# A streaming encoder step: gate and residual of the second MLP applied behind the last but one group of its down projection

## The chip, the cores and the metric

The kernel runs on one core of a Trainium2 chip. A core has TensorE (matrix products into PSUM, 8 banks), VectorE, ScalarE and GpSimd (element-wise work), and SyncE, whose queue issues most of the DMAs; GpSimd and ScalarE can issue DMAs too. 16 DMA engines carry the transfers of all queues. The metric is the device time of one execution, in microseconds. In the profile PE is TensorE, DVE is VectorE, ACT is ScalarE, POOL is GpSimd, SP is SyncE; L1443 is line 1443 of the kernel, and a group is written "out<-in" with the program's names for tiles.

## The reference, cut to what matters

One inference step of a two-layer encoder on 1056 tokens (1024 of a prompt and 32 of a sample, each of the two with its own conditioning), 1024 features, 4096 hidden features in the MLP. Each layer ends with a squared-ReLU MLP whose result is scaled by a gate per feature and condition and added to the residual, before a layer norm:

```python
u = x * (1 + sc2) + sh2
f = jnp.square(jax.nn.relu(u @ p['w_up'][l])) @ p['w_down'][l]
x = layer_norm(ALPHA * x + (1 + g2) * f, p['ln_g'][l, 1], p['ln_b'][l, 1])
```

Here `g2` differs between the 1024 prompt tokens and the 32 sample tokens. Everything is float32; the kernel computes products as three passes over a high and a low part of each operand. The factor 1/ALPHA is folded into the gate, so that in the kernel the sum is `x + gate * f`.

## The kernel before, in words

Features lie on partitions, tokens along the free dimension. An accumulator `ACX` of two tiles, four blocks of 128 features each (index `fc`, 0 to 7), holds all 1056 tokens. Tokens are cut into four quarters of `QN` = 264; the last quarter holds the last 232 prompt tokens and the 32 sample tokens.

The second MLP (`mlp7(L1)`) runs the hidden features in 16 blocks of 256. For the first 14 the products are made by a scheme of seven products in place of eight (`PRODS`): per product a weight form (from `forms`: sums and differences of quarter blocks of the weights, split into a high and a low part) and a form of the hidden activations, which the up projection has written to DRAM (`hd`). The last two blocks are multiplied plainly at the end.

The down projection of the 14 blocks goes in five groups (`GRP`, of 2, 3, 3, 3 and 3 blocks, numbered 0 to 4) of four units each; a unit `(g, m)` makes two feature blocks, `fc` = 2m and 2m+1, for all tokens: seven products times two halves of the tokens (`tp`), fourteen in all, each of 9 matmuls of 264 columns in groups 1 to 4. Their sums stay in PSUM banks within the unit (`unit`, L1428 to 1449). After each product one quarter of one feature block is complete enough to be taken out: `L.raw` (that is `add_raw_at`) copies it into `ACX` on ScalarE for the first product that touches the place (group 0), and adds it there on VectorE otherwise (L1066, one instruction of 128 x 264). The bank is free again when that is done.

What goes on beside a unit:

- `step` calls `advance` after each product: the weights of the next units are loaded (`rdn_d`, two loads of 384 KB a unit, L1256, on SyncE's queue), added and subtracted on VectorE (L1272 to 1275) and split by ScalarE's cast (L89) and VectorE's subtraction (L90) into `wf_d`. The loads go through a ring of three buffers, the split weights through one of six.
- in the last unit of a group, `after` hands the place of each used activation form to the next group's (`fill`, `rooms`): its DMA (`fx`, `fx_e`, `fx_w`, L1124, 792 KB for each of the fourteen operands, in one or two pieces) goes onto SyncE's queue behind the product that frees the place. A few operands are loaded earlier into free places.
- after each unit of the last group, 4, `L.fold` (that is `gate_raw`) is called for the two feature blocks: ScalarE multiplies them by the gate (L1073: 1024 prompt columns, then 32 sample columns), and an accumulating DMA on GpSimd's queue (L1074, 528 KB) adds the residual from DRAM (`xsp[2]`) to them.

Behind the last unit the remaining two blocks are multiplied plainly (L118 to 120, `dn_plain`'s counterpart at the end of `mlp7`): operands `hs` (four loads of 1056 KB, L1553), weights `w_dn` (four loads of 512 KB, L96), and each product goes into `ACX` by `L.add` (that is `add_gated_at`, L1057): `ACX = product * gate + ACX`, on VectorE, one instruction for each condition that the columns cover. Then the layer norm and the output follow, token block by token block.

The order on TensorE is written out by hand (`manual_schedule`). On the other engines the instructions are ordered by the framework's planner from the order of the program and its own costs; each engine and each queue then works in that order, and a waiting instruction holds what is behind it.

Of the kernel before, what the change touches and what calls it, by code (L numbers as in the profile page):

```python
# [75 lines left out]
def trunk_kernel(ctx: ExitStack, tc: tile.TileContext, a, o):  # L76
# [100 lines left out]
    def tpt(name):  # L177
        return pa.tile([P, 512], F32, tag="tp", name=name, bufs=2)
# [27 lines left out]
    tp = tpt("tp_c")  # L206
# [13 lines left out]
    tp = tpt("tp_p2")  # L220
# [876 lines left out]
    QN = T // 4  # L1097
    NPB, KG = 16, 4
    GRP = [(0, 2), (2, 3), (5, 3), (8, 3), (11, 3)]
# [31 lines left out]
    def mlp7(L):  # L1131
# [212 lines left out]
        def advance(n, i):  # L1344

            if n + 1 in preps and i in (0, 1, 3, 5):
                got[n + 1] = next(preps[n + 1])
            if i == 2:
                prep(n + 2)
            if not NW and n == len(seq) - 1 and i in (1, 3):  # L1350
                w_plain(0, i // 2)
# [65 lines left out]
        def fill(g, into, most=99):  # L1417

            kg = GRP[g][1]
            while want and len(rooms.free) >= kg and most:  # L1420
                most -= 1
                if g >= len(GRP) - 3:
                    late = g == len(GRP) - 1 or g == len(GRP) - 2 and len(into) < 10
                    rooms.free.sort(key=lambda r: any(r[0] is t for t in f4s[:3]) == late)
                tp, f = want.pop(0)
                into[tp, f] = rooms.load(hd[g][tp][f], kg)

        def unit(g, m, phases, ws, step, after):  # L1428


            kg = GRP[g][1]
            for tps in phases:
                ps = {}
                for i, (w, f, b, c, q) in enumerate(PRODS):
                    for tp in tps:
                        first = (tp, b) not in ps
                        if first:
                            ps[tp, b] = mm(f"dn{l}_{g}_{m}_{tp}_{b}")
                        p = ps[tp, b][:, :QN]
                        for k in range(kg):  # L1440
                            t, s0 = fx[tp, f][k]
                            for n_, (wl, xl) in enumerate(((0, 0), (0, 1), (1, 0))):
                                nc.tensor.matmul(p, ws[w][:, wl, k], t[:, s0, xl], start=first and k + n_ == 0,  # L1443
                                                 stop=k == kg - 1 and n_ == 2, skip_group_check=not first)
                        L.raw((2 * tp + q) * QN, QN, p, 2 * m + c, g == 0 and i in (0, 2, 3, 6))
                        after(tp, f)
                        flow.tick(QN * kg / 768)
                    if tps is phases[-1]:
                        step(i)
# [16 lines left out]
        with tc.manual_schedule(engines={mybir.EngineType.PE}):  # L1466
            for _, j, i in sorted((7 * j + 2 * i, j, i) for j in range(len(jobs)) for i in range(7)):
                n, tp = jobs[j]
# [53 lines left out]
        with tc.manual_schedule(engines={mybir.EngineType.PE}):  # L1522
            for i, (g, m, phases) in enumerate(units):
                more = g + 1 < len(GRP)
                if i == 0:
                    rooms.add(ring.tile([P, KG, 2, QN], F32R, tag="wc", name=f"fx_w{l}", bufs=6))
                    fill(0, fx)
                if m == 1 and more:
                    want += [(tp, f) for f in order_f for tp in L.pairs]
                if g and m == 2 and more:  # L1530
                    fill(g + 1, nfx)

                def after(tp, f):
                    if m == 3 and more:
                        rooms.free += fx[tp, f]
                        fill(g + 1, nfx)

                def step(j):
                    advance(nu + i, j)
                    if g == 0 and m in (1, 2):  # L1540
                        fill(g + 1, nfx, 1)
                unit(g, m, phases, got[nu + i], step, after)
                if not more:
                    for fc in (2 * m, 2 * m + 1):
                        L.fold(L.gate, fc, xsp[2])
                if m == 3:
                    assert not want
                    fx, nfx = nfx, {}
# [68 lines left out]
    class L0:  # L1617
# [46 lines left out]
        def after(blk):  # L1664
# [3 lines left out]
            norms[ti] = flow.add(norm(ti, 1, f"n01_{ti}", W01[ti], False, lambda ti: acc_dma(  # L1668
                xsp[1][:, :, t0:t0 + n], acc[ti], True)), now=NOW)
    mlp7(L0)  # L1670


# [8 lines left out]
    for gi, grp in enumerate(((0, 1, 2), (3,))):  # L1681
        ws = {pr: [wblock(f"q{pr}_{half}", wq, 512 * half, 256 * pr) for half in range(2)] for pr in grp}
        for ti, (t0, n) in enumerate(TBS):
# [9 lines left out]
            for fc in [f for pr in grp for f in (2 * pr, 2 * pr + 1)]:  # L1693
                g, r = fc // 2, 2 * (fc % 2)
# [217 lines left out]
    for gp in range(2):  # L1912
        for i in range(17):
            c = slim[gp][i // 2] if i % 2 else wide[i // 2] if i < 16 else slim[gp][8]
            if not gp and i < 2:
                c = 7 + i
# [18 lines left out]
    for t in range(NT):  # L1935
# [4 lines left out]
        m = P if t < NT - 1 else TS  # L1940
# [124 lines left out]
    class L1:  # L2065
# [49 lines left out]
        def after(blk):  # L2115
            t0, n = blk
            tiles = [(t, min(P, t0 + n - t)) for t in range(t0, t0 + n, P)]
            flow.add(norm_out(tiles, L1.put_out, L1.next_y, L1.gb, blk == L1.blocks[-1]), TAIL[0])
    mlp7(L1)
    flow.finish()  # L2120
    psD_cm.__exit__(None, None, None)
# [36 lines left out]
```

## Time and profile before

| | us |
|---|---|
| median of 3 runs (2407.66 to 2410.68) | 2410.06 |
| the profiled execution | 2410.77 |
| its span, first to last instruction | 2409.0 |
| TensorE busy | 2341.5 (97%) |
| VectorE busy | 1935.2 (80%) |
| ScalarE busy | 1206.4 (50%) |
| GpSimd busy | 176.3 (7%) |

The mean granted clock of TensorE is 0.995 of full speed. Of the profile these views are used: the page; rows of stretches of time (busy time of each engine with its count of instructions, then the granted clock `PEclk`, the share of the 16 DMA engines and what they moved in GB/s); timelines (start, duration, engine, line, operation, and in brackets how long the engine was idle before it and what ended that); the chain of waits that ended last (start, duration, what); and the DMA view (a queue with its packets, megabytes and share of 16 engines; an issue with its size and the time to landing). q1 is the queue of SyncE's DMAs, q0 that of GpSimd's. A busy TensorE is modelled, so its rows tell when it stood still, and the length of a unit tells how fast it was.

The last group's folds stand in the profile at 2283.7 to 2340.0 (ScalarE, 16 activations) and 2288.1 to 2341.6 us (GpSimd, 8 DMAs); the plain blocks begin at 2339.3.

### The profile page before, as it was taken

Reading aid. Unit: us, or ns where it says so; the run is one execution under the profiler, and the core shown is the slowest. Engines: PE = TensorE matmul, PEld = TensorE weight load, DVE = VectorE, ACT = ScalarE, POOL = GpSimd, SP = SyncE. Lnnn points to the kernel's source line nnn. Section 1 sums busy time; section 2 is a strip of 40 time slices with the busy share of each in tenths; the row PEclk is TensorE's granted clock in tenths of the full one; section 3 lists DMA queues with packets and bytes.
Section 4 is the critical chain, followed back from the end, with each engine's and each line's share of the span. In section 5 each row is a group of like instructions: output and inputs, shape, how many; then the busy total and the mean of one; then the engine's idle time right before and its main releaser. Section 6 shows DMA issues by size and latency. Waiting matters only on the chain. (4 is left out here: it accounts for less than half of the span.)

```text
span 2409.0 us, 44246 instructions
## 1 busy us (share of the span) xinstructions
PE 2341.5 (97%) x17180; PEld 2250.1 (93%) x17180; DVE 1935.2 (80%) x3982; ACT 1206.4 (50%) x2442; POOL 176.3 (7%) x323
## 2 busy tenths in 40 slices
PE   7999999999999999999999999999999999999997
PEld 4999999999999999999989987789999999999997
DVE  4899897778788789989888677757998889677658
ACT  4644457278566631000147467764766777422232
POOL 0211100000000000000000224420000000000013
PEclk9999999999999999999999999999999999999999
DMA  8333322526566896675512230051586789866672
GB/s 302 120 113 95 100 84 79 173 97 203 182 202 198 287 350 238 226 272 204 177 62 88 77 93 1 19 134 56 175 279 207 254 279 313 328 244 240 237 191 74
DMA packets 284854, 424.65 MB, mean 176 GB/s; under 512 B 15448, under 2 KB 205292, under 8 KB 280036
## 3 DMA queue, kind: packets, MB, share of 16 engines
q1 hardware_dynamic: 279284, 387.15, 48.5%
q10 hardware_dynamic: 4208, 30.35, 3.2%
q0 software_dynamic: 1152, 4.33, 1.0%
q8 instruction: 135, 2.21, 0.4%
q14 instruction: 75, 0.61, 0.1%
HBM read 305.96 MB, written 118.17 MB: 176 GB/s over the span
## 5 line engine op out<-in xcount | busy, mean ns | idle before, releaser
L1443 PE MATMUL dn<-fx,wf_d 128*128 128x264 f32 x2016 | 254.7, 286 | 6.9 <-DVE ACX L1066 3.1
L1443 PEld LDWEIGHTS dn<-fx,wf_d 128*128 128x128 f32 x2016 | 250.0, 189 | 8.5 <-issue 3.0
L89 ACT CAST w_dn<-raw_dn 128x1024 fp32r<-128x1024 f32 x36 | 37.7, 1050 | 285.1 <-DMA raw_dn<-in_w_down_dram 111.8
L1057 DVE SCALAR_TENSOR_TENSOR ACX<-dn,ada,ACX 128x384 f32<-128x384 f32 (+5 forms) x304 | 136.9, 469 | 40.0 <-PE dn L120 37.2
L118 PE MATMUL dn<-hs,w_dn 128*128 128x384 f32 (+2 forms) x512 | 160.9, 315 | 0.0
L119 PE MATMUL dn<-hs,w_dn 128*128 128x384 f32 (+2 forms) x512 | 160.9, 315 | 0.0
L120 PE MATMUL dn<-hs,w_dn 128*128 128x384 f32 (+2 forms) x512 | 156.4, 314 | 1.3 <-DVE w_dn L90 1.3
L1066 DVE TENSOR_TENSOR ACX<-dn,ACX 128x264 f32<-128x264 f32 x248 | 104.4, 429 | 62.3 <-PE dn L1443 60.9
L1308 PE MATMUL up<-TF,wf_u 128*128 128x264 f32 x1056 | 143.2, 285 | 4.1 <-ACT H L1311 4.1
L1308 PE MATMUL up<-U,wf_u 128*128 128x264 f32 x1056 | 139.6, 285 | 1.1 <-DVE H L1314 0.7
L1308 PE MATMUL up<-u,wf_u 128*128 128x264 f32 x1056 | 139.4, 284 | 1.2 <-DVE H L1314 0.8
L277 DVE SCALAR_TENSOR_TENSOR aw<-radw,cs,aw 128x512 f32<-128x512 f32 x196 | 139.3, 742 | 1.4 <-DMA radw<-in_w_ada_dram 1.4
L1308 PEld LDWEIGHTS up<-TF,wf_u 128*128 128x128 f32 x1056 | 134.2, 188 | 5.1 <-ACT H L1311 5.1
L1308 PEld LDWEIGHTS up<-U,wf_u 128*128 128x128 f32 x1056 | 133.1, 188 | 2.1 <-DVE H L1314 1.3
L1308 PEld LDWEIGHTS up<-u,wf_u 128*128 128x128 f32 x1056 | 132.5, 188 | 1.8 <-DVE H L1314 1.2
L118 PE MATMUL dn<-U,w_dn 128*128 128x384 f32 (+2 forms) x416 | 129.4, 312 | 0.9 <-DVE ada L302 0.9
L119 PE MATMUL dn<-U,w_dn 128*128 128x384 f32 (+2 forms) x416 | 129.8, 313 | 0.0
L120 PE MATMUL dn<-U,w_dn 128*128 128x384 f32 (+2 forms) x416 | 125.5, 312 | 0.4 <-DVE w_dn L90 0.4
L1811 ACT ACTIVATE p<-p,mx 128x576 f32<-128x576 f32 (+9 forms) x132 | 86.5, 656 | 27.1 <-DVE mx L1808 24.9
L90 DVE TENSOR_TENSOR HL<-H,HL 128x1056 fp32r<-128x1056 f32 x64 | 80.3, 1254 | 22.7 <-ACT HL L89 22.3
L120 PEld LDWEIGHTS dn<-hs,w_dn 128*128 128x128 f32 x512 | 95.9, 188 | 2.1 <-DVE w_dn L90 1.7
L119 PEld LDWEIGHTS dn<-hs,w_dn 128*128 128x128 f32 x512 | 96.5, 188 | 0.0
(399 smaller groups left out, 7249.2 us busy)
## 6 DMA issues: line engine op xcount, KB each, us to landing
hpl<-HL SPq DMA_DIRECT2D x144, 264.0 KB
rdn_u<-in_w_up_dram SPq DMA_DIRECT2D x64, 512.0 KB
hd<-HL SPq DMA_DIRECT2D x28, 1056.0 KB
fx<-hd SPq DMA_DIRECT2D x50, 528.0 KB
radw<-in_w_ada_dram SPq DMA_DIRECT2D x24, 1024.0 KB
hd<-HM SPq DMA_DIRECT2D x28, 792.0 KB
raw_up<-in_w_up_dram SPq DMA_DIRECT2D x40, 512.0 KB
raw_dn<-in_w_down_dram SPq DMA_DIRECT2D x36, 512.0 KB
```

Source lines behind the costliest of these rows:

```text
L89: nc.scalar.copy(dst_h, src)
L90: (eng or nc.vector).tensor_sub(dst_l, src, dst_h.bitcast(F32))
L118: nc.tensor.matmul(ps, wh, mov(0, k), start=(k == 0), stop=False)
L119: nc.tensor.matmul(ps, wh, mov(1, k), start=False, stop=False)
L120: nc.tensor.matmul(ps, wl, mov(0, k), start=False, stop=(k == nk - 1))
L277: nc.vector.scalar_tensor_tensor(acc[cnd], raw[:, k], sc, acc[cnd], op0=ALU.mult, op1=ALU.add)
L1057: nc.vector.scalar_tensor_tensor(xs, ps[:, off + o:off + o + mm_], gate[:, fc, cnd:cnd + 1], xs, op0=ALU.mult, op1=ALU.add)
L1066: nc.vector.tensor_add(x[:, fc], ps[:, off:off + m], x[:, fc])
L1308: nc.tensor.matmul(p, self.ws[w][:, wl, k], moving(f, tp, xl, k), start=first and k + n_ == 0, stop=k == 3 and n_ == 2, skip_group_check=n ...
L1443: nc.tensor.matmul(p, ws[w][:, wl, k], t[:, s0, xl], start=first and k + n_ == 0, stop=k == kg - 1 and n_ == 2, skip_group_check=not first)
L1811: nc.scalar.activation(z, z, AF.Exp, bias=mx[:, 0:1], scale=-1.0, accum_out=mx[:, 1:2])
```

## The change

The fold of a pair of feature blocks is called behind the unit of group 3 that makes them, and no longer behind that of group 4. At that time `ACX` holds the sum of groups 0 to 3, so gate and residual are applied to this; the products of group 4 are then added with the gate, by the function that the plain blocks use. In the last quarter of the tokens that function issues two instructions (232 and 32 columns), so that four of a unit's fourteen additions become two each.

```diff
                                 nc.tensor.matmul(p, ws[w][:, wl, k], t[:, s0, xl], start=first and k + n_ == 0,
                                                  stop=k == kg - 1 and n_ == 2, skip_group_check=not first)
-                        L.raw((2 * tp + q) * QN, QN, p, 2 * m + c, g == 0 and i in (0, 2, 3, 6))
+                        if g < len(GRP) - 1:
+                            L.raw((2 * tp + q) * QN, QN, p, 2 * m + c, g == 0 and i in (0, 2, 3, 6))
+                        else:
+                            L.add((2 * tp + q) * QN, QN, p, L.gate, 2 * m + c)
                         after(tp, f)
...
                 unit(g, m, phases, got[nu + i], step, after)
-                if not more:
+                if g == len(GRP) - 2:
                     for fc in (2 * m, 2 * m + 1):
                         L.fold(L.gate, fc, xsp[2])
```

The two functions called, as they were:

```python
def add_gated_at(t0, n, ps, gate, fc):
    for off, m, x in pieces(t0, n):
        for o, mm_, cnd in segs(t0 + off, m):
            xs = x[:, fc, o:o + mm_]
            nc.vector.scalar_tensor_tensor(xs, ps[:, off + o:off + o + mm_], gate[:, fc, cnd:cnd + 1], xs,
                                           op0=ALU.mult, op1=ALU.add)

def gate_raw(gate, fc, src):
    x = acc["all"].tiles[fc // 4][:, fc % 4]
    for off, m, cnd in segs(0, T):
        xs = x[:, off:off + m]
        nc.scalar.activation(xs, xs, AF.Copy, scale=gate[:, fc, cnd:cnd + 1])
    nc.gpsimd.dma_start(x, src[:, fc], accum_op=ALU.add)
```

## The prediction

> **What bounds the kernel now.** First the page of the kernel before: its span, its engines, and the group of additions that the change is about.
>
> ```profile
> span 2409.0 us, 44246 instructions
> PE 2341.5 (97%) x17180; PEld 2250.1 (93%) x17180; DVE 1935.2 (80%) x3982; ACT 1206.4 (50%) x2442; POOL 176.3 (7%) x323
> L1066 DVE TENSOR_TENSOR ACX<-dn,ACX 128x264 f32<-128x264 f32 x248 | 104.4, 429 | 62.3 <-PE dn L1443 60.9
> ```
>
> TensorE sets the pace, so an edit counts only where it lengthens or shortens a unit of the second down projection. I write (g,m) for group g, unit m; the change touches groups 3 and 4, the last two. A unit without a stall is 126 matmuls in 15.36 us. Counting back from the last matmul of (4,3), whose end is at 2339.4, the view of stretches gives one row for each of the eight units, (3,0) to (4,3):
>
> ```profile
> core 0: us, PE busy (x) PEld busy (x) DVE busy (x) ACT busy (x) POOL busy (x), PEclk, DMA share, GB/s
> 2211.45:2226.81 15.36, 15.36 (x129) 15.36 (x128) 12.03 (x28) 3.40 (x7) 0.00 (x0) 1.00 0.84 327
> 2226.81:2242.17 15.36, 15.36 (x129) 15.36 (x128) 11.67 (x27) 3.29 (x7) 0.00 (x0) 1.00 0.57 193
> 2242.17:2257.53 15.36, 15.36 (x129) 15.36 (x128) 10.87 (x25) 3.29 (x7) 0.00 (x0) 1.00 0.18 52
> 2257.53:2272.89 15.36, 15.36 (x129) 15.36 (x128) 9.37 (x21) 3.30 (x7) 0.00 (x0) 1.00 0.97 351
> 2272.89:2288.25 15.36, 15.36 (x129) 15.36 (x128) 11.51 (x26) 5.10 (x10) 0.19 (x1) 1.00 0.94 354
> 2288.25:2307.25 19.00, 17.43 (x129) 17.03 (x128) 12.05 (x28) 5.93 (x11) 1.72 (x2) 0.91 0.75 213
> 2307.25:2322.61 15.36, 15.36 (x129) 15.36 (x128) 9.37 (x21) 6.05 (x11) 1.92 (x3) 1.00 0.62 140
> 2322.61:2339.41 16.80, 15.56 (x128) 15.37 (x127) 9.97 (x18) 6.95 (x8) 1.57 (x2) 1.00 0.76 198
> ```
>
> Six units run at the pace; (4,1) is 3.64 us longer and (4,3) 1.44 us, 5.08 us together, and those are the two stalls that can be won. The timeline of VectorE (first three rows), of GpSimd, of the DMA queue of SyncE and the chain of waits tell what they hang on:
>
> ```profile
> 2275.50 0.55 DVE L1272 TENSOR_TENSOR s_d<-rdn_d,rdn_d 128x384 f32<-128x384 f32 x1
> 2300.97 0.56 DVE L1272 TENSOR_TENSOR s_d<-rdn_d,rdn_d 128x384 f32<-128x384 f32 x1 [4.53 <-DMA rdn_d<-in_w_down_dram]
> 2335.34 1.23 DVE L90 TENSOR_TENSOR w_dn<-raw_dn,w_dn 128x1024 fp32r<-128x1024 f32 x1 [3.45 <-ACT w_dn L89]
> ...
> 2288.06 1.04 POOL L1074 DMA_DIRECT2D ACX<-xsp  x1 [693.38 <-ACT ACX L1073]
> 2290.65 0.86 POOL L1074 DMA_DIRECT2D ACX<-xsp  x1 [1.54 <-ACT ACX L1073]
> 2325.16 0.86 POOL L1074 DMA_DIRECT2D ACX<-xsp  x1 [1.84 <-ACT ACX L1073]
> ...
> 2291.62 9.26 DMA rdn_d<-in_w_down_dram
> 2325.04 9.12 DMA raw_dn<-in_w_down_dram
> 2135.37 5.40 DMA rdn_d<-in_w_down_dram
> ```
>
> The chain is one of data: in (4,1) a 384 KB weight load issued at 2291.62 takes 9.26 us, where the same load took 5.40 us earlier in the phase; VectorE stands 4.53 us at the head of its queue waiting for it (L1272), the additions that empty the PSUM banks stand behind it, and TensorE runs out of banks. In (4,3) a 512 KB load takes 9.12 us, ScalarE's cast of it is late, and VectorE idles 3.45 us. Beside each late load run two accumulating DMAs of the fold (the folds of (4,0) at 2288.06 and 2290.65, one of (4,2) at 2325.16). What a fold takes of the DMA engines is in the DMA view from 2288 to 2301 (first four rows), and what plain loads take in the one from 2259 to 2282.5 (last row):
>
> ```profile
> q1 hardware_dynamic: 999, 2.33, 55.7%
> q0 software_dynamic: 288, 1.08, 41.8%
> hs<-hpl SPq DMA_DIRECT2D x2, 1056.0 KB
> ACX<-xsp POOLq DMA_DIRECT2D x2, 528.0 KB, 9.6
> ...
> q1 hardware_dynamic: 3603, 8.81, 101.1%
> ```
>
> 41.8% of 13 us is 5.43 us of all 16 engines for two folds: 2.7 us each, 5.0 us per MB. 101.1% of 23.5 us over 8.81 MB is 2.7 us per MB for plain loads. A fold therefore costs nearly twice its bytes, and whatever load shares the engines with two of them is up to 5.4 us late.
>
> **The change part by part.** *The folds move up by one group.* The 8 folds (16 activations on ScalarE, 8 DMAs on GpSimd's queue) are issued 61.4 us (4 x 15.36) before where they would stand without stalls, one pair behind each of (3,0) to (3,3). By the offset of the pair of (4,0) from its unit's start (15.2 and 17.8 us), the pairs are then issued at about 2226.6/2229.2, 2242.0/2244.6, 2257.4/2260.0 and 2272.7/2275.3. ScalarE has room: busy 3.3 us of 15.36 in these units. GpSimd's queue holds nothing else there.
>
> *Group 4 loses them.* The load at 2291.62 and that at 2325.04 get the engines back. 9.26 less up to 5.4 is 3.9, so the nearest value is the 5.40 us of the quiet one: landing some 4 us sooner, the 4.53 us wait is nearly gone, and 9.12 less one or two folds takes the 3.45 us off too. I take the whole 5.08 us as won; the lower end is 3.64, if (4,3) stalls for its 1 MB `hs` load and not for the fold.
>
> *(3,3) and (4,0) get them.* These are the units in which the operands of group 4 are loaded, and the DMA is full there: share 0.97 and 0.94 above. SyncE's queue in that stretch, with three rows of ScalarE's, the last two from the end of (4,0):
>
> ```profile
> 2258.31 0.34 SPq L1124 DMA_DIRECT2D fx_e<-hd  x1
> 2258.70 0.90 SPq L1124 DMA_DIRECT2D fx<-hd  x2
> 2259.77 0.32 SPq L1124 DMA_DIRECT2D fx_e<-hd  x1
> 2260.51 5.28 SPq L1124 DMA_DIRECT2D fx<-hd  x8
> 2267.32 0.38 SPq L1256 DMA_DIRECT2D rdn_d<-in_w_down_dram  x1
> 2267.80 7.50 SPq L1124 DMA_DIRECT2D fx<-hd  x8
> ...
> 2274.93 0.51 ACT L89 CAST wf_d<-rdn_d 128x384 fp32r<-128x384 f32 x1 [1.47 <-DMA rdn_d<-in_w_down_dram]
> 2288.36 0.93 ACT L89 CAST wf_d<-rdn_d 128x384 fp32r<-128x384 f32 x2 [0.62 <-PE dn L1443]
> 2289.19 1.15 ACT L1073 ACTIVATE ACX<-ACX,ada 128x1024 f32<-128x1024 f32 x1
> ```
>
> The 20 `fx` issues are ten operands of 792 KB, used by the last ten products of (4,0), and in the middle of them stands the second weight load for (4,1) (2267.32). It lands at 2274.93, and VectorE comes to its L1272 at 2275.50: 0.57 us to spare. The pair of (3,2) falls into the queue's work ahead of it and adds 5.4 us; of the pair of (3,3) the first (2272.7) adds 2.7, the second I leave out, since behind (4,0) the second gate (2289.19) stands on ScalarE after the casts of the weight loads (2288.36), and behind (3,3) one of these waits for this very load. Landing: 2274.93 + 8.1 = 2283.0, and VectorE waits 7.5 us at L1272 with the additions of (4,0) behind it. Bounds: 4.8 us (pair of (3,2) alone) and 10.3 us (all four). Waits of 4.53 and 3.45 us cost 3.64 and 1.44 us before, so a wait costs itself less 0.9 to 2.0 us; with the 0.9 of the longer one, 7.5 becomes 6.6 us, and the bounds 2.8 and 9.4. The last operand tells about the same: ten times 0.81 MB and the 0.39 MB weight load at 2.7 us per MB are 23 us, from about 1 us behind the first issue, 2259.3, to 2282.3, and its product starts at 2288.25 - 1.1 = 2287.15, so 8.1 us more make it 3.3 us late; with TensorE already late, that hides in the 6.6 us.
>
> *The same in (3,1) and (3,2).* The weight loads there go out at 2228.04 and 2243.40, each beside its unit's pair of folds, but with an otherwise emptier DMA (0.57 and 0.18). In the timeline VectorE waits 0.88 us for the second, and that is its longest wait of the kind in these units:
>
> ```profile
> 2246.83 0.56 DVE L1272 TENSOR_TENSOR s_d<-rdn_d,rdn_d 128x384 f32<-128x384 f32 x1 [0.88 <-DMA rdn_d<-in_w_down_dram]
> ```
>
> At worst one fold goes ahead of each: 2.7 us of wait at most in the first, 3.6 in the second, and less the 2.0 us of the shorter wait that is 0 to 0.7 and 0 to 1.6 us. Taken: 0.7 for both; bounds 0 and 2.3.
>
> *56 additions become gated ones.* The rows by shape, of which the group's ungated row stands above at 429 ns:
>
> ```profile
> L1057 DVE SCALAR_TENSOR_TENSOR ACX<-dn,ada,ACX 128x32 f32<-128x32 f32 x72 | 17.3, 240 | 0.0
> L1057 DVE SCALAR_TENSOR_TENSOR ACX<-dn,ada,ACX 128x264 f32<-128x264 f32 x24 | 11.4, 482 | 3.1 <-PE dn L120 3.1
> L1057 DVE SCALAR_TENSOR_TENSOR ACX<-dn,ada,ACX 128x232 f32<-128x232 f32 x8 | 3.6, 445 | 0.0
> L1057 DVE SCALAR_TENSOR_TENSOR ACX<-dn,ada,ACX 128x288 f32<-128x288 f32 x8 | 4.1, 518 | 8.7 <-PE dn L120 8.7
> ```
>
> In each unit of group 4 four of the 14 products land on the last quarter, which holds the 32 sample columns and is split: 10 x 482 + 4 x (445 + 240) = 7.56 us against 14 x 429 = 6.01, so 1.55 us more of VectorE a unit and 16 instructions more in all. In units that run at the pace VectorE idles 3.3 us or more (12.03 of 15.36 busy at most), and that hides it. Where VectorE catches up behind its late load in (4,0), it is bare: 0 to 1.55, taken 0.5.
>
> *The end.* The last two folds no longer stand between (4,3) and the plain blocks. The first block's eight additions (128x288, last row above) name TensorE alone in their waits, no fold, so nothing is won there: 0 to 0.1 us.
>
> **The sum**, against the profiled execution: -5.08 + 6.6 + 0.5 + 0.7 = +2.7 us on 2410.77, that is 2413.5. The median of the runs shown is 2410.06, 0.7 lower, so I forecast 2412.8 us for it. By its bounds this case runs from -5.08 + 2.8 = -2.3 to -3.64 + 9.4 + 1.55 + 2.3 = +9.6; its likely part is 2409 to 2416.
>
> **The rivals.** *The folds are absorbed* (17%): the queue's order or VectorE's shifts so that L1272 comes after the load, and the 4.9 us to the last operand's use cover most of it. For it: there is no wait for an operand in any unit before. Against it: 0.57 us to spare at L1272 and a DMA with no gap. What is left is -5.08 + 0.7 = -4.4: 2405.7 us. The Trainium skill has a rule that points this way ("DMA: Bandwidth & Descriptors", Anatomy of one DMA — SWDGE path): a DMA takes 2.0 us plus its bytes over 436 GB/s, which for the 541 KB of a fold is 1.24 us of movement; three folds would then delay the weight load by 3.7 us, the wait would be 3.1 us, the unit's loss about 1 us, and the time about 2407 (an estimate by that page). The trace differs: 2.7 us of all engines for each accumulating fold.
>
> *Slower* (23%): all four folds of (3,2) and (3,3) go ahead of the weight load, in (4,0). The wait is 10.3 us, the unit loses 9.4 and 1.55 for the gated additions in the catch-up, (3,1) and (3,2) take 1.6: -5.08 + 12.55 = +7.5, 2417.6 us. It decides from a wait of about 9.6 us at (4,0)'s L1272, where the sum passes +4.8 with the other terms as forecast (-5.08 + 9.6 - 0.9 + 1.2). For it: the loads on SyncE's queue go in order, and the DMA has no gap to catch up in. Against it: the last gate's place on ScalarE.
>
> *The change does not do what it says* (6%): the old stalls belong to the 1 MB `hs` loads that run beside them, so group 4 keeps its 5.08 us while (4,0) pays 7.1: +7.8, 2417.9 us. Against it: the folds held 5.4 of the 9.26 us.
>
> **How the numbers follow.** 54% for the forecast, 17%, 23% and 6% for the rivals. A measurement of this kernel can tell about 0.2%, 4.8 us, from no change. Slower by more: 29% of the rivals and a tenth of the forecast's own case, 0.34. Faster by more: half of the absorbed case, 0.09. The rest, 0.57, is within. For the range I take half of the absorbed case in and the slower ones to 2419: 2405 to 2419.
>
> **What would show it.** Right: (4,1) and (4,3) at 15.4 us; (4,0) longer than 19 us with VectorE waiting 5 to 10 us for `rdn_d` around 2276 and a lower granted clock behind it; the pairs on GpSimd's queue near the eight times given; 0.48 us for the gated additions and no idle TensorE from them. Wrong: (4,0) at 15.4 us (absorbed), or a (4,1) still at 19 us (no fold's doing).

## The result, and the profile after

The changed kernel takes 2423.8 us (median of 5 runs, 2421.31 to 2425.8), the kernel before 2410.29 us in the runs beside it (5 runs, 2407.66 to 2413.64): a ratio of 1.0054, with a 95% interval of 1.0039 to 1.0069. It is 13.5 us slower, where the prediction had 2.7 us more than the median shown and a range that ended at 2419. The profiled execution of it took 2422.23 us. First the page's span and engines, and the group of additions without the gate:

```profile
span 2420.5 us, 44267 instructions
PE 2342.7 (97%) x17180; PEld 2250.8 (93%) x17180; DVE 1939.7 (80%) x3998; ACT 1204.8 (50%) x2442; POOL 175.7 (7%) x323
L1066 DVE TENSOR_TENSOR ACX<-dn,ACX 128x264 f32<-128x264 f32 x192 | 80.7, 429 | 47.3 <-PE dn L1443 47.1
```

The change is in: 56 of the 248 plain additions are gone, there are 16 instructions more on VectorE, and the busy time of no engine has moved by more than 5 us. The 11.5 us of span are standing time. The stretches of the eight units (3,0) to (4,3) say where:

```profile
core 0: us, PE busy (x) PEld busy (x) DVE busy (x) ACT busy (x) POOL busy (x), PEclk, DMA share, GB/s
2210.54:2225.90 15.36, 15.36 (x129) 15.36 (x128) 11.95 (x28) 5.09 (x10) 0.20 (x1) 1.00 0.87 334
2225.90:2246.00 20.10, 17.15 (x129) 16.93 (x128) 11.49 (x27) 6.04 (x11) 1.89 (x3) 0.92 0.71 201
2246.00:2262.91 16.91, 15.59 (x129) 15.41 (x128) 10.59 (x25) 6.04 (x11) 1.70 (x3) 1.00 0.55 111
2262.91:2278.27 15.36, 15.36 (x129) 15.36 (x128) 9.37 (x21) 6.05 (x11) 1.76 (x3) 1.00 0.97 275
2278.27:2304.82 26.55, 17.35 (x128) 17.17 (x127) 12.56 (x30) 4.55 (x8) 1.58 (x2) 0.81 0.97 330
2304.82:2320.18 15.36, 15.36 (x128) 15.36 (x127) 13.61 (x32) 3.30 (x7) 0.00 (x0) 1.00 0.53 193
2320.18:2335.54 15.36, 15.36 (x128) 15.36 (x127) 10.71 (x25) 3.30 (x7) 0.00 (x0) 1.00 0.23 69
2335.54:2350.92 15.38, 15.38 (x128) 15.38 (x127) 11.48 (x22) 4.10 (x4) 0.00 (x0) 1.00 0.43 144
```

(4,1) and (4,3) are back at the pace: the 5.08 us are won. (3,1) loses 4.74 us, (3,2) 1.55 and (4,0) 11.19. That is +17.5 - 5.1 = +12.4 us in the eight units (140.4 us, before 128.0); the phase began 0.9 us earlier than before, which leaves the +11.5 of the span. Three rows each of VectorE's timeline, of TensorE's (all the stalls it has in these units) and of the chain of waits show what the three units hang on:

```profile
2237.79 0.56 DVE L1272 TENSOR_TENSOR s_d<-rdn_d,rdn_d 128x384 f32<-128x384 f32 x1 [5.49 <-DMA rdn_d<-in_w_down_dram]
2253.81 0.56 DVE L1272 TENSOR_TENSOR s_d<-rdn_d,rdn_d 128x384 f32<-128x384 f32 x1 [4.02 <-DMA rdn_d<-in_w_down_dram]
2291.46 0.56 DVE L1272 TENSOR_TENSOR s_d<-rdn_d,rdn_d 128x384 f32<-128x384 f32 x1 [10.44 <-DMA rdn_d<-in_w_down_dram]
...
2238.75 7.29 PE L1443 MATMUL dn<-fx,wf_d 128*128 128x264 f32 x45 [2.95 <-DVE ACX L1066]
2256.13 6.81 PE L1443 MATMUL dn<-fx,wf_d 128*128 128x264 f32 x54 [1.32 <-DVE ACX L1066]
2296.26 11.54 PE L1443 MATMUL dn<-fx,wf_d 128*128 128x264 f32 x78 [9.20 <-ACT wf_d L89]
...
2227.13 10.57 DMA rdn_d<-in_w_down_dram
2247.25 6.46 DMA rdn_d<-in_w_down_dram
2278.57 12.87 DMA rdn_d<-in_w_down_dram
```

It is the mechanism of the forecast, three times over: a weight load beside accumulating DMAs lands late, VectorE stands at L1272, the PSUM banks or the split weights run out. The wait in (4,0) is 10.44 us, where 7.5 were forecast, and its price is more than the wait. Two things made the load that late. Its issue, on SyncE's queue:

```profile
2265.99 11.27 SPq L1124 DMA_DIRECT2D fx<-hd  x8
2278.57 0.38 SPq L1256 DMA_DIRECT2D rdn_d<-in_w_down_dram  x1
2279.05 12.77 SPq L1124 DMA_DIRECT2D fx<-hd  x8
```

The eight `fx` issues ahead of it took 11.27 us where they took 5.28 before. The view of waits of that queue (us in total, times, longest) names earlier `fx` loads that had not landed, first in the changed kernel from 2262 to 2292, then in the kernel before from 2257 to 2283:

```profile
SPq L1124 <- DMA fx<-hd: 9.2, 5, 3.0
...
SPq L1124 <- DMA fx<-hd: 4.1, 7, 1.1
```

The trace shows why. The program gives SyncE's loads here eight semaphores (counters that a landing raises) in turn, and an issue that takes one waits until the load that had it before has landed. The weight load takes that of the first of the eight `fx` loads. That one landed 6.44 us behind its issue before (2260.51 to 2266.95), and 12.22 us behind it now (2265.99 to 2278.21); the weight load went out 0.4 us behind either. So the load stands 15.66 us behind the start of (3,3) (2278.57 - 2262.91) instead of 9.80 (2267.32 - 2257.52). From issue to landing it then took 12.87 us instead of 7.61. 5.86 + 5.26 is 11.1 us later in its unit; the forecast had 8.1. And both folds of (3,3) are ahead of its landing, as the rows of GpSimd (the pair of (3,0), the first fold of (3,2), the pair of (3,3)) and of ScalarE show:

```profile
2225.70 1.04 POOL L1074 DMA_DIRECT2D ACX<-xsp  x1 [630.67 <-DMA fx<-hd]
2228.28 0.86 POOL L1074 DMA_DIRECT2D ACX<-xsp  x1 [1.55 <-ACT ACX L1073]
...
2262.77 0.87 POOL L1074 DMA_DIRECT2D ACX<-xsp  x1 [13.43 <-ACT ACX L1073]
...
2278.11 0.86 POOL L1074 DMA_DIRECT2D ACX<-xsp  x1 [11.89 <-ACT ACX L1073]
2280.36 0.88 POOL L1074 DMA_DIRECT2D ACX<-xsp  x1 [1.40 <-ACT ACX L1073]
...
2278.80 1.15 ACT L1073 ACTIVATE ACX<-ACX,ada 128x1024 f32<-128x1024 f32 x1
2291.46 0.51 ACT L89 CAST wf_d<-rdn_d 128x384 fp32r<-128x384 f32 x1 [11.51 <-DMA rdn_d<-in_w_down_dram]
```

The second gate (2278.80) stands ahead of the cast that waits for the load (2291.46), not behind it.

### The profile page after: what moved, and what is told of

It reads as the page before. It is cut to its first block, busy times and chain, and to the rows that moved or that the text cites. A ratio compares the mean times of both kernels' runs of the same rounds, so it can differ in the third digit from the quotient of the medians.

```text
span 2420.5 us, 44267 instructions
## 1 busy us (share of the span) xinstructions
PE 2342.7 (97%) x17180; PEld 2250.8 (93%) x17180; DVE 1939.7 (80%) x3998; ACT 1204.8 (50%) x2442; POOL 175.7 (7%) x323
## 5 line engine op out<-in xcount | busy, mean ns | idle before, releaser
L1057 DVE SCALAR_TENSOR_TENSOR ACX<-dn,ada,ACX 128x256 f32<-128x256 f32 (+6 forms) x376 | 166.2, 462 | 52.3 <-PE dn L120 37.4
L1066 DVE TENSOR_TENSOR ACX<-dn,ACX 128x264 f32<-128x264 f32 x192 | 80.7, 429 | 47.3 <-PE dn L1443 47.1
L1814 ACT ACTIVATE p<-p,mx 128x576 f32<-128x576 f32 (+9 forms) x132 | 86.5, 656 | 27.1 <-DVE mx L1811 25.0
```

The source lines that it names most:

```text
L1057: nc.vector.scalar_tensor_tensor(xs, ps[:, off + o:off + o + mm_], gate[:, fc, cnd:cnd + 1], xs, op0=ALU.mult, op1=ALU.add)
L1066: nc.vector.tensor_add(x[:, fc], ps[:, off:off + m], x[:, fc])
L1814: nc.scalar.activation(z, z, AF.Exp, bias=mx[:, 0:1], scale=-1.0, accum_out=mx[:, 1:2])
```

## The experiments

In what follows a unit's length is measured from the same point of one unit to that of the next. Without stalls the eight units take 122.8 us; the kernel before took 127.9, the changed one 140.3 (the rows above add up to 0.1 us more, since they run to the end of the last matmul).

**The gated additions.** The changed kernel with plain additions in group 4; its output lacks the gate on that group's products.

```diff
-                        if g < len(GRP) - 1:
-                            L.raw((2 * tp + q) * QN, QN, p, 2 * m + c, g == 0 and i in (0, 2, 3, 6))
-                        else:
-                            L.add((2 * tp + q) * QN, QN, p, L.gate, 2 * m + c)
+                        L.raw((2 * tp + q) * QN, QN, p, 2 * m + c, g == 0 and i in (0, 2, 3, 6))
```

> The changed kernel with plain additions in group 4 in place of the gated ones: the folds stay behind group 3's units, and the products of group 4 are added without the gate, so the output lacks the gate on the last three blocks of the MLP. Theory A (the accumulating DMAs of the folds delay the weight loads): nothing but VectorE's 1.55 us a unit goes, so 2422 to 2425 us, (4,0) still 25 to 27 us long. Theory B (the gated additions and their 16 more instructions fill VectorE): back to 2405 to 2411 us.

Measured: 2422.12 us (2421.37 to 2423.55; the kernel before beside it 2407.17), ratio 1.0062 (1.0047 to 1.0077). The units take 140.0 us with TensorE's three stalls at 2.83, 1.46 and 9.07 us, close to the changed kernel's 2.95, 1.32 and 9.20. The gated additions cost nothing that can be measured.

**The accumulating DMAs, away.** The changed kernel and the kernel before, each without the eight DMAs of L1074; their outputs lack the residual.

```diff
-            nc.gpsimd.dma_start(x, src[:, fc], accum_op=ALU.add)
```

> The changed kernel without the accumulating DMAs: gates on ScalarE and gated additions stay where they are, the residual is not added, so the output lacks it. Theory A (DMAs): all eight units of groups 3 and 4 at 15.4 us, except for a stall of the gates' own; 2411 less 5.1 = 2405 us, and VectorE waits under 1 us for a weight load. Theory C (the gates stand in ScalarE's queue ahead of the casts, and the planner's new order does the rest): the time stays at 2418 to 2424 us.

> The kernel before without its accumulating DMAs (output without the residual). Theory A: (4,1) and (4,3) come down to 15.4 us each, 5.1 us less: 2405 us. If the 1 MB loads of the last blocks' operands made those two stalls instead: 2409 to 2411 us, with (4,1) still near 19 us.

Measured: the changed kernel 2404.4 us (ratio to the kernel before 0.9988, 0.9979 to 0.9998), the kernel before 2403.47 (0.9985, 0.9975 to 0.9994). In both the eight units take 122.8 us and TensorE has no stall in them. In the changed kernel without the DMAs, ScalarE, VectorE and SyncE work through these units in the same order, instruction by instruction, as with them. So the eight DMAs, and not the gates, the additions or another order of instructions, make both the 17.5 us that the change lost and the 5.08 us that it won. (By the medians the eight DMAs cost the kernel before 3.7 us, 1.4 to 6.0.) The rival by which the `hs` loads made the old stalls is out: those loads are all still there.

**The same bytes without accumulating.** The changed kernel, its eight DMAs copying the residual over `ACX` instead of adding it; the output lacks what `ACX` held.

```diff
-            nc.gpsimd.dma_start(x, src[:, fc], accum_op=ALU.add)
+            nc.gpsimd.dma_start(x, src[:, fc])
```

> The changed kernel with the same eight DMAs on the same queue, but copying the residual over the accumulator in place of adding to it (the output loses the sums of groups 0 to 3). A DMA of 0.54 MB then takes 1.5 us of all engines at the 2.7 us per MB of plain loads, where the accumulating one takes 2.7. Theory A with the delay in proportion to engine time: the waits at L1272 shrink to a little over half (10.4 us to 6, 5.5 to 3, 4.0 to 2), and the loss by about 10 us: 2411 to 2416 us. If only the number of packets in turn counts and not their duration: no change, 2421 to 2425 us.

Measured: 2409.6 us (2404.69 to 2415.5, wide), ratio 1.0005 (0.9994 to 1.0016). In its profiled run the units take 124.1 us, and one stall is left, 1.10 us in (4,0). The view of DMA queues from 2225 to 2238 us of the changed kernel, then from 2223 to 2235 of this one (queue, packets, MB, share of 16 engines):

```profile
q0 software_dynamic: 288, 1.08, 43.1%
```

```profile
q0 software_dynamic: 288, 1.08, 23.1%
```

43.1% of 13 us is 5.6 us for two accumulating DMAs, 2.8 us each; 23.1% of 12 us is 2.8 us for two plain ones, 1.4 us each. The same bytes in as many packets hold the engines for half as long, and of the 17.5 us lost in the units 1.3 are left in this execution. That misses the expectation: the waits at L1272 in (3,1), (3,2) and (4,0) fell to 1.37, 2.01 and 2.34 us, not to 3, 2 and 6, so here they fell by more than the engines' time. But this execution is the fastest of the ten, and the median is 5.2 us above that of the kernel without the DMAs (2404.4). So the direction is shown, and the size is open.

**Which folds cost what: halves of the change.** Once the folds of units 0 and 1 alone are moved up, once those of units 2 and 3 alone (in each, the gated additions go with them).

```diff
-                        if g < len(GRP) - 1:
+                        if g < len(GRP) - 1 or m > 1:
...
-                if g == len(GRP) - 2:
+                if g == (len(GRP) - 2 if m < 2 else len(GRP) - 1):
```

> The change for the first two units of a group alone: the folds of m = 0 and 1 stand behind (3,0) and (3,1), with gated additions in (4,0) and (4,1); those of m = 2 and 3 stay behind (4,2) and (4,3). Theory (each pair delays the weight load that is under way in the unit behind it, and nothing else): (3,1) keeps its loss of about 4.7 us and (3,2) its 1.6 us, (4,0) and (4,1) run at 15.4 us, (4,3) keeps 1.4 us; -3.64 + 4.74 + 1.55 = +2.7 us on the kernel before, about 2413 us. Rival (the loss in (4,0) is a backlog that the stalls of (3,1) and (3,2) leave in SyncE's queue): (4,0) stays near 26 us long and the time near 2424 us.

> The change for the last two units of a group alone: the folds of m = 2 and 3 stand behind (3,2) and (3,3), with gated additions in (4,2) and (4,3); those of m = 0 and 1 stay behind (4,0) and (4,1). Theory (the four folds of two pairs delay the one weight load in (4,0)): (3,1) and (3,2) at 15.4 us, (4,0) near 26.5 us, (4,1) keeps a loss of up to 3.6 us, (4,3) loses nothing; -1.44 + 11.2 = +9.8 us, about 2420 us, or 2416 us if (4,1) has recovered its time in the long (4,0). Rival (backlog of the stalls of (3,1) and (3,2)): (4,0) is at most 5 us long of the pace, and the time is below 2414 us.

| unit, us | (3,1) | (3,2) | (3,3) | (4,0) | (4,1) | (4,2) | (4,3) | all eight |
|---|---|---|---|---|---|---|---|---|
| before | 15.4 | 15.4 | 15.4 | 15.4 | 19.0 | 15.4 | 16.7 | 127.9 |
| changed | 20.1 | 16.9 | 15.4 | 26.6 | 15.4 | 15.4 | 15.3 | 140.3 |
| first half up | 20.1 | 16.9 | 15.4 | 15.4 | 15.4 | 15.4 | 15.3 | 129.1 |
| second half up | 15.4 | 15.4 | 15.4 | 27.1 | 17.3 | 15.4 | 15.2 | 136.5 |

Measured: first half 2410.58 us (ratio 1.001, 1.0001 to 1.002, beside 2407.98 for the kernel before), second half 2417.81 us (1.0039, 1.0026 to 1.0052). Each unit pays for the folds beside it: the first half makes the losses of (3,1) and (3,2) and none in (4,0), the second half the one of (4,0) alone. The rival by which (4,0) inherits a backlog from (3,1) and (3,2) falls. Two misses, and with them both times are some 2 us under the expected 2413 and 2420: in the first half (4,3) loses nothing although its folds stand where they stood before, and in the second (4,1) loses 2.0 us instead of 3.6. The first can be followed to the last weight load. ScalarE's cast of it, in the kernel before and with the first half up, where (4,3) starts at 2322.61 and 2324.94:

```profile
2334.25 1.05 ACT L89 CAST w_dn<-raw_dn 128x1024 fp32r<-128x1024 f32 x1 [5.19 <-DMA raw_dn<-in_w_down_dram]
...
2333.82 1.05 ACT L89 CAST w_dn<-raw_dn 128x1024 fp32r<-128x1024 f32 x1 [2.43 <-PE dn L1443]
```

In both the load is issued 2.43 us behind the start of the unit, and the folds of (4,2) 0.17 us ahead of that start and 2.55 behind it. Yet the cast comes 11.6 us behind the start in the one, held by the load, and 8.9 in the other, where the load is in already. So the spacing of fold and load alone doesn't fix the delay.

**Which pair makes the wait in (4,0).** The changed kernel with the DMAs of one pair only: that of (3,2), then that of (3,3) (`fc in (6, 7)`). The residual of the other six blocks is left out. Lines below L1074 stand one later, L1273 for L1272.

```diff
-            nc.gpsimd.dma_start(x, src[:, fc], accum_op=ALU.add)
+            if fc in (4, 5):
+                nc.gpsimd.dma_start(x, src[:, fc], accum_op=ALU.add)
```

> The changed kernel with only the two accumulating DMAs of the pair of (3,2) (feature blocks 4 and 5); the residual of the other six blocks is left out of the output. By the prediction's own terms (5.4 us for a pair, 0.57 us to spare): VectorE waits 4.8 us at L1272 in (4,0), and the unit loses 3.9 to 5 us; (3,1) and (3,2) at the pace; the time 2403.5 + 4 to 5 = about 2408 us. If the wait of 10.4 us comes from the late issue on SyncE's queue, and that from this pair, the issue of the weight load stands 15 to 16 us behind the start of (3,3) here too, and the wait is 5 to 6 us. If the pair has no part in it, (4,0) is at 15.4 us and the time 2404 us.

> The changed kernel with only the two accumulating DMAs of the pair of (3,3) (feature blocks 6 and 7); the residual of the other six blocks is left out. By the prediction's own terms only one of the two is ahead of the weight load: a wait of 2.7 - 0.57 = 2.1 us, a loss of about 1 us, 2404.5 us. If both go ahead of it as the traces now say: a wait of 4.8 to 5.3 us, a loss of 4 to 5 us, about 2408 us, with the issue of the weight load at 9.8 us behind the start of (3,3) as in the kernel before. If this pair alone makes the whole wait: 10 us and 2414 us.

The rows of SyncE's queue and of VectorE's and TensorE's timelines with the pair of (3,2), where (3,3) starts at 2255.10:

```profile
2258.09 11.33 SPq L1125 DMA_DIRECT2D fx<-hd  x8
2270.69 0.38 SPq L1257 DMA_DIRECT2D rdn_d<-in_w_down_dram  x1
...
2279.68 0.56 DVE L1273 TENSOR_TENSOR s_d<-rdn_d,rdn_d 128x384 f32<-128x384 f32 x1 [6.46 <-DMA rdn_d<-in_w_down_dram]
...
2284.48 12.22 PE L1444 MATMUL dn<-fx,wf_d 128*128 128x264 f32 x78 [5.22 <-ACT wf_d L89]
```

And with the pair of (3,3), where (3,3) starts at 2254.13:

```profile
2257.12 5.80 SPq L1125 DMA_DIRECT2D fx<-hd  x8
2264.27 0.38 SPq L1257 DMA_DIRECT2D rdn_d<-in_w_down_dram  x1
...
2272.74 0.56 DVE L1273 TENSOR_TENSOR s_d<-rdn_d,rdn_d 128x384 f32<-128x384 f32 x1 [0.49 <-DMA rdn_d<-in_w_down_dram]
...
2286.05 3.93 PE L1444 MATMUL dn<-fx,wf_d 128*128 128x264 f32 x30 [0.68 <-DMA fx<-hd]
```

Measured: 2409.64 us (ratio 1.0007, 0.9996 to 1.0017) and 2406.76 us (0.9992, 0.9982 to 1.0003). From the start of (3,3), all in us:

| | issue of the load | landing | wait at its first sum | loss of (4,0) |
|---|---|---|---|---|
| before | 9.8 | 17.4 | none | 0 |
| pair of (3,2) alone | 15.6 | 24.6 | 6.46 | 7.9 |
| pair of (3,3) alone | 10.1 | 18.6 | 0.49 | 2.2 |
| both pairs, second half up | 15.9 | 28.6 | 10.48 | 11.7 |
| all four, changed | 15.7 | 28.6 | 10.44 | 11.2 |

The late issue is the work of the pair of (3,2) alone. That pair makes the landing 7.2 us later (forecast 5.4). The pair of (3,3) does 1.2 us by itself, since the load then leaves early and is nearly in before those folds start (its own loss of 2.2 us is 0.56 us of waiting for a bank, 0.68 for a late operand, and slower matmuls behind them), and 4.0 us (forecast 2.7) behind the other, when the late load runs into them. The two pairs' effects do not simply add up: 7.2 + 1.2 against 11.1. By the prediction's own terms the two runs were to lose 4 to 5 and about 1 us in (4,0); they lost 7.9 and 2.2.

**A version in which no load is late.** If the folds cost only where a load that is due soon shares the engines, the kernel before can keep them behind group 4 and hold the harmful ones. Here the gates of (4,0)'s pair read a copy of the gate that depends on the sum of the last unit's weight load, and those of (4,2)'s pair one that depends on the last split plain weights, so their DMAs start only then (`sums` collects the first sum of each weight load, `g_late` is the copy). The output is unchanged.

```diff
-                if not more:
+                if not more and m in (1, 3):
                     for fc in (2 * m, 2 * m + 1):
                         L.fold(L.gate, fc, xsp[2])
...
+        def fold_after(src, m):
+            nc.vector.scalar_tensor_tensor(g_late[:, 2 * m:2 * m + 2], src, 0.0, L.gate[:, 2 * m:2 * m + 2],
+                                           op0=ALU.mult, op1=ALU.add)
+            for fc in (2 * m, 2 * m + 1):
+                L.fold(g_late, fc, xsp[2])
...
+                    if (g, m, j) == (4, 2, 1):
+                        fold_after(sums[-1][:, 0:2, 0:2], 0)
...
+        fold_after(ws[3][:, 1, 0:2, 0:2].bitcast(F32), 2)
```

> The kernel before, with its folds behind group 4, but two of its pairs held: the gate of the pair of (4,0) is made to depend on the sum of the last unit's weight load (L1272 for (4,3)), and that of the pair of (4,2) on the last split plain weights, so that their accumulating DMAs start when no weight load is under way. Output unchanged. Theory (an accumulating DMA costs time only where a load that VectorE waits for shares the engines with it): both stalls of the kernel before go, (4,1) and (4,3) at 15.4 us, and if the last folds do not delay the plain blocks the time is 3.5 to 5 us below the kernel before, 2404 to 2406 us. Rival 1 (the last folds, later now, hold up the plain blocks or the layer norm behind them): no gain or a loss, 2408 to 2412 us. Rival 2 (the pairs of (4,1) and (4,3) make stalls of the same size): same time as before.

Measured: 2403.01 us (11 runs, 2401.43 to 2405.41; the kernel before beside it 2407.19), ratio 0.9982 (0.9973 to 0.9991). Its units (4,0) to (4,3), and the stretch of the plain blocks behind them:

```profile
2268.18:2283.53 15.35, 15.35 (x129) 15.35 (x128) 11.36 (x26) 3.40 (x7) 0.00 (x0) 1.00 0.96 359
2283.53:2298.89 15.36, 15.36 (x129) 15.36 (x128) 12.40 (x30) 5.50 (x11) 0.00 (x0) 1.00 0.57 194
2298.89:2314.24 15.35, 15.35 (x129) 15.35 (x128) 9.36 (x21) 6.24 (x12) 3.68 (x4) 1.00 0.97 209
2314.24:2329.46 15.22, 15.22 (x127) 15.22 (x126) 10.21 (x19) 7.72 (x10) 0.88 (x1) 1.00 0.41 148
2329.46:2344.00 14.54, 14.54 (x114) 14.54 (x113) 3.02 (x6) 1.72 (x3) 2.61 (x3) 1.00 1.00 216
```

In (4,2) four accumulating DMAs fill the engines (0.97), and the unit runs at the pace. Two 512 KB weight loads go out beside them, at 2297.95 and 2300.45, but ScalarE's first cast of them, at 2314.35, waits for TensorE and not for a load: the folds cost the unit nothing where no load is due. The eight units take 122.6 us, 5.2 less than before. Part is given back at the end: from the first plain matmul (2329.46) to the end of the span (2401.2) it takes 71.7 us, where the kernel before took 69.7 (2339.33 to 2409.0), and the chain of waits names the last fold for it:

```profile
2336.71 8.19 DMA ACX<-xsp
```

The layer norm waits for that block. 5.24 - 2.07 is 3.2 us, within the interval of the medians' 4.2 us (2.2 to 6.5). (The profiled executions differ by more, 7.8 us, because the phase began 4.6 us earlier in this one, at 2206.8 instead of 2211.5; across the eleven traces here it begins anywhere between the two.) This version is faster than the kernel before by 0.1 to 0.3%, and so faster than the changed one.

## Why the prediction was wrong

*What held.* Group 4 got its 5.08 us back, whole. The gated additions are as long as forecast, 488 ns for 482, by the group of the changed kernel's 264-column ones, and cost nothing of the time:

```profile
L1057 DVE SCALAR_TENSOR_TENSOR ACX<-dn,ada,ACX 128x264 f32<-128x264 f32 x64 | 31.0, 488 | 12.0 <-PE dn L1443 8.4 <-PE dn L120 3.1
```

At the end of the phase nothing moved: 69.65 us from the first plain matmul (2350.85) to the end of the span, before 69.67. The folds were placed as forecast: by the start of their units, (3,2)'s pair went out 16.8 us after it (2262.77 - 2246.00, where the unit itself is 1.55 us longer), and the cost per accumulating DMA was 2.8 us against 2.7. The wait was at L1272 for `rdn_d`, with a lower clock behind it.

*Where it failed*, by the terms of the sum:

| term | forecast | measured |
|---|---|---|
| group 4 loses the folds | -5.08 | -5.08 |
| (4,0) | +6.6 and 0.5 | +11.2 |
| (3,1) and (3,2) | +0.7 | +6.3 |
| sum of the units | +2.7 | +12.4 |

1. *(3,1) and (3,2), 5.6 us too small: the largest error.* The step was "At worst one fold goes ahead of each", and it failed in (3,1). The load there is issued at 2227.13, between the folds at 2225.70 and 2228.28, and takes 10.57 us. Before, it took 5.2 us at most, since VectorE passed its L1272 at 2233.19 without waiting, 5.15 us behind the issue. So it came at least 5.4 us later, about what two folds hold the engines for: by that, the one issued 1.15 us behind the load delayed it as well. VectorE waits 5.49 us, where 2.7 was the most. In (3,2), with the same spacing and an otherwise emptier DMA, the load came 3.1 us later, about one fold, and the wait was 4.02 us, where 3.6 was the most. The price was then put 2.0 us below the wait: (3,1) lost 4.74 of its 5.49, while the 1.55 of (3,2) lie inside its bounds of 0 to 1.6. The first half of the change, run alone, made the same two losses (4.7 and 1.5 us).

2. *The second fold of (3,3) was left out.* The step was that its gate "stands on ScalarE after the casts of the weight loads". It came before the cast that waits (2278.80 against 2291.46). The place was read from the order behind (4,0), and behind (3,3) another order was compiled. With both folds of it in, the prediction's own arithmetic gives the wait of 10.3 us that the slower rival had, and 10.44 was measured. That they agree so well is partly luck: the arithmetic takes 5.4 us for each pair, and the pairs made the landing 7.2 and 4.0 us later.

3. *The load's own issue was taken as fixed.* 2267.32 was carried over, and the late issue is 5.9 of the 11.1 us. SyncE's queue does not pass its eight `fx` issues in 5.28 us while the pair of (3,2) takes the engines: 11.33 us with that pair alone, 5.80 without it. The load goes out only when the `fx` load eight issues ahead of it has landed, and that took 12.2 to 12.6 us from its own issue in the three versions with both folds of (3,2) behind their unit, and 6.4 to 6.8 in the kernel before, without the DMAs, with the first half up and with the pair of (3,3) alone. The forecast's "adds 5.4 us" for this pair, put on the landing, caught most of it by another name.

4. *From wait to loss the sign was wrong in (4,0).* The step was that "a wait costs itself less 0.9 to 2.0 us", from two stalls in which TensorE ran out of banks. In (4,0) it runs out of the split weights themselves (9.20 us, `wf_d`), so only 1.2 of VectorE's 10.44 us is covered; and behind the stall TensorE is slow. At the pace a matmul takes 15.36/126 = 0.122 us, 78 of them 9.5 us; the row at 2296.26 has 11.54. 9.20 + 2.0 = 11.2, the loss. In (3,1) it is 2.95 + (7.29 - 45 x 0.122) = 4.75.

So the rival that ended slower had the right mechanism and, with the luck of point 2, the right wait in (4,0). Its loss there, 9.4 and 1.55 for the gated additions, comes near the 11.2 measured, but the 1.55 stood for something that cost nothing, and the slow clock that made up for it was not in it. Its 2417.6 us is too low because it took (3,1) and (3,2) at 1.6 us, where they lost 6.3. The rival "absorbed" is refuted: neither SyncE's order nor VectorE's moved in the change's favour. By the figure that the prediction quoted from the Trainium skill ("DMA: Bandwidth & Descriptors", Anatomy of one DMA — SWDGE path), 1.24 us of movement for a fold, the estimate was 2407. The plain DMAs come near that figure with 1.4 us, and the kernel with them took 2409.6; the accumulating ones took 2.8.

*What stays open.* Why the last weight load of (4,3) lands sooner when only the first half is moved up, with the folds at the same distance from it; and by how much plain DMAs would delay the loads, since that kernel's runs scatter over 11 us.

## What to carry to other kernels

Price a moved DMA at each place where it lands, by what is in flight there, in time and not in bytes: an accumulating DMA here held the engines for 2.8 us per 0.54 MB. In the changed kernel the weight loads of (3,1) and (3,2), each beside two of them, landed at least 5.4 and 3.1 us later than before. Ask also what the load's own issue waits for: in (4,0) it was the landing of the load eight issues ahead, which the folds had slowed, and the weight load landed 11.1 us later. Look first for a stretch in which no load is due soon: in the version with the folds held, four at once cost their unit nothing beside two loads, the first of which was used 16 us behind its issue. And a stall's price is read from what runs out: TensorE stood 2.2 to 3.0 us less than VectorE waited where it ran out of banks (four stalls), and 1.2 us less where it ran out of operands (10.44 and 6.46 us of wait); the slow clock behind the stalls added 0.2 to 2.7 us.

## What the runs showed of the hardware that was not expected

The granted clock goes to half in or behind a stall, and stays there after TensorE is back at work. The changed kernel's rows around the long stall:

```profile
2292.00:2294.00 2.00, 0.00 (x0) 0.00 (x0) 2.00 (x6) 1.02 (x2) 0.00 (x0) 0.50 1.06 427
2296.00:2298.00 2.00, 1.74 (x8) 1.77 (x9) 2.00 (x7) 0.00 (x0) 0.00 (x0) 0.50 1.04 395
2298.00:2300.00 2.00, 2.00 (x11) 2.00 (x11) 1.03 (x3) 0.00 (x0) 0.00 (x0) 0.50 1.09 365
2302.00:2304.00 2.00, 2.00 (x19) 2.00 (x18) 1.41 (x5) 0.51 (x1) 0.00 (x0) 1.00 0.35 139
```

A row counts 11 matmuls in 2 us where it counts 19 at full clock (those that cross its edges are counted too). What the slow clock costs is not in proportion to the stall: by the lengths of the matmul groups, 2.0 us behind 9.20, 2.7 behind 5.22, 1.8 behind 2.95. Short stalls go either way. The kernel before, with 1.56 us of stall in (4,1), then the second half up, with 1.45 us in the same unit and the same 51 matmuls behind it:

```profile
2301.93 8.26 PE L1443 MATMUL dn<-fx,wf_d 128*128 128x264 f32 x51 [1.56 <-DVE ACX L1066]
```

```profile
2311.39 6.73 PE L1443 MATMUL dn<-fx,wf_d 128*128 128x264 f32 x51 [1.45 <-DVE ACX L1066]
```

At the pace these take 51 x 0.122 = 6.2 us: the one stall cost 2.0 us more than itself, the other 0.5. The granted clock agrees: over (4,1) it is 0.91 in the kernel before, where it falls to half some 2 us behind the stall, and 1.00 with the second half up. The row of the kernel before:

```profile
2304.00:2306.00 2.00, 2.00 (x11) 2.00 (x11) 1.57 (x4) 0.73 (x3) 0.00 (x0) 0.50 0.03 8
```

So nearly all of the difference between the 3.6 us that (4,1) lost before and the 2.0 it lost there is the clock, not the wait; two stalls do not make a rule for where it decides.

The Trainium skill ("TensorE: Matmul & The Clock Gate", Part 1: The HAM clock gate) has the clock fall to half after an idle window of about 3.4 us, watched by a counter that runs freely, and come back after about 3.4 us of work. The time back agrees roughly: at half rate, 2.0 us lost are 4 us of work, and 5.4 us in the kernel with the pair of (3,2) alone (12.22 us for 78 matmuls, 2.7 us lost). The first part doesn't agree as a threshold on the stall: 1.56 us were enough here.
